# Two heads by turns: reordering the small attention matmuls of a decoder block

## The chip, the core and the metric

The kernel runs on one core of a Trainium2 chip. TensorE (PE in the rows, PEld for its weight loads), VectorE (DVE), ScalarE (ACT), GpSimdE (POOL) and the DMA queues started by SyncE (SP) each run a queue of their own and meet at semaphores. The metric is the device time of one execution in microseconds. Over three runs the kernel before took 1109.73, 1112.56 and 1114.26 us, median 1112.56.

## The reference, cut to what matters

One decoder layer over 256 tokens of width 1024, in float32: a conditioned norm, an input projection, two attentions that are gated and merged, an output projection, then an expert network in which every token meets 16384 experts' grid, and a last norm. The change touches only the two attentions. Both have heads of 64 columns.

```python
# stick-breaking attention, 8 heads
z = einsum('bqhd,bkhd->bhqk', qb, kb) * scale            # scores, contraction over 64
log_1m_beta = where(mask, log_sigmoid(-z), 0)
after = cumsum(log_1m_beta, reverse=True) - log_1m_beta
a = where(mask, exp(log_sigmoid(z) + after), 0)
out = einsum('bhqk,bkhd->bqhd', a, vb)                   # weighted values, 64 columns out
...
# dilated attention, 4 heads in each of 3 groups, softmax over the three groups' keys together
z = einsum('bqhd,bqnhd->bhqn', qb, kg) * scale
out = einsum('bhqn,bqnhd->bqhd', softmax(z), vg)
```

## The kernel before, in words

Everything dense runs as three float32r matmuls per product (a high and a low part of each operand; helper `mm3`, lines 85 to 87), whose weights come from DRAM in blocks of 512 KB (`unit`); ACT copies the high part out (line 81) and DVE subtracts to get the low part (line 82). A gate projection `gates(b)` is two such blocks, 48 matmuls.

The attentions use plain float32 matmuls, which the trace shows as two matmul records each. Two heads of 64 rows lie in one 128-partition tile: an even head in partitions 0 to 63, an odd one in 64 to 127.

- `stick_a(p)`, for a pair p of four: the scores of two heads go to two PSUM banks of one tile `z`. For each head a bf16 matmul over all 128 rows writes the mask (line 358), then the scores add to it: one float32 matmul with 256 moving columns (line 359) and one with 128 (line 363), both on the 64 rows of the head. The second head follows when the first is done.
- `stick_b(p)` adds the running sums (lines 377, 378), full-size float32 matmuls.
- `stick_c(p)`: weighted values, 64 output columns per head, so head 0 writes partitions 0 to 63 of the tile `po` and head 1 partitions 64 to 127 (lines 388, 392). Head 0's two matmuls come first in the code, then head 1's, with nothing between.
- `dilated(h, o)`, for one head at a time: for each half `tt` of the queries the masks (line 404, or 407 and 408), three score matmuls on the head's 64 rows (line 411) with 128 or 256 moving columns, the softmax (DVE maximum line 417, ACT exponential line 421, DVE scaling line 423), transposes in threes (line 428) that ACT copies out (line 429), and three or six weighted-value matmuls with 64 output columns (line 433) into the head's half of the tile `o`. The scores' tile is one of two buffers of pool `pz`, which the projections of the values (`proj_v`) use too; the transposes' tile and `o` share two buffers of pool `pm`, so the transposes have one of them.

At the end of the attention stage a loop takes two pairs of dilated heads; after each head come two gate projections and, with `bg`, one step of background work on DVE.

A planner at build time lays out each engine's queue. It takes instructions by their place in the code, but passes over those that it reckons not to be ready, so that the transposes stand in the trace amid the gate projections that follow them in the code.

Of the kernel before, what the change touches and what calls it, by code (L numbers as in the profile page):

```python
# [7 lines left out]
F32 = mybir.dt.float32  # L8
# [4 lines left out]
AF = mybir.ActivationFunctionType  # L13
# [11 lines left out]
# activations of the first J0 columns of experts are worked out while the routing goes on and kept in DRAM  # L25
J0 = 116
# steps of the routing, and batches of gates, to a pair of such columns
PACE_R = 2.5
PACE_G = 2.0
# the first norm's scales (even) and shifts (odd) that the tensor engine works out  # L30
# [4 lines left out]
def kernel(  # L35
# [60 lines left out]
    def rsqrt(r, m, q, n=1):  # L96
        # 1 / sqrt(m) for n columns, halves m: first guess from the exponent, then Newton steps to float32's
        # accuracy
        nc.vector.tensor_scalar(r.bitcast(I32), m.bitcast(I32), 1, None, op0=OP.arith_shift_right)
        nc.vector.tensor_scalar(  # L100
            r.bitcast(I32), r.bitcast(I32), -1, 0x5F3759DF, op0=OP.mult, op1=OP.add
        )
        nc.vector.tensor_scalar(m, m, -0.5, None, op0=OP.mult)
        for _ in range(3):
            for i in range(n):
                c = slice(i, i + 1)
                nc.vector.scalar_tensor_tensor(q[:, c], r[:, c], r[:, c], m[:, c], op0=OP.mult, op1=OP.mult)
            for i in range(n):
                c = slice(i, i + 1)
                nc.vector.scalar_tensor_tensor(r[:, c], q[:, c], 1.5, r[:, c], op0=OP.add, op1=OP.mult)  # L110
# [51 lines left out]
    def ada1(k):  # L162
        # scale and shift of row block k; some from the weights as they come on the tensor engine
        raw = spool.tile([P, 2, D], F32, tag="ada", bufs=3, name=f"ada1_{k}")
        nc.sync.dma_start(raw, w_ada[2 * k : 2 * k + 2].rearrange("k p d -> p k d"))
        got = []
        for i in range(2):
            t = 2 * k + i
            if t in ON_PE:
                row = pp.tile([1, P], F32, tag="pp", name=f"row_{t}")  # L170
                wk = raw[:, i].rearrange("p (k n) -> p k n", k=NC8)
                for j in range(NC8):
                    nc.tensor.matmul(row, cc[:, j : j + 1], wk[:, j], start=(j == 0), stop=(j == NC8 - 1))
                rs = spool.tile([1, P], F32, tag="rs", bufs=2, name=f"rs_{t}")
                nc.scalar.activation(rs, row, AF.Copy, scale=-1.0)
                cm = pm.tile([P, 1], F32, tag="mm", name=f"cm_{t}")
                nc.tensor.matmul(cm, rs, neg_one[0:1, 0:1], start=True, stop=True)
                got.append(cm)
            else:
                dots(raw[:, i : i + 1], t)  # L180
                got.append(mod[:, t : t + 1])
        g, b = gs[:, 0, k : k + 1], mod[:, 2 * k + 1 : 2 * k + 2]
        nc.vector.scalar_tensor_tensor(
            g, got[0], bcol1[:, k : k + 1], gcol[:, 0, k : k + 1], op0=OP.add, op1=OP.mult
        )
        nc.vector.tensor_add(b, got[1], bcol[:, 2 * k + 1 : 2 * k + 2])
        return g, b
# [10 lines left out]
    def rms(sq, name):  # L198
        # 1 / rms with tokens on partitions, then along them on all partitions
# [37 lines left out]
    # the first column blocks, for q and k, take each row block of h as its modulation arrives  # L237
# [72 lines left out]
    def roped(dst, ps, name):  # L310
        t1 = spool.tile([P, 2, T], F32, tag="att", bufs=6, name=f"t1_{name}")
        t2 = spool.tile([P, 2, T], F32, tag="att", bufs=6, name=f"t2_{name}")
        nc.vector.tensor_mul(t1, ps, rp[:, 0:1].to_broadcast([P, 2, T]))
        nc.vector.tensor_mul(t2, ps, rp[:, 1:2].to_broadcast([P, 2, T]))
        # rows of a pair of tiles: heads 0 2 1 3; two heads of 64 rows to each tile that is kept
        for i in range(2):
            nc.vector.tensor_sub(dst[:, i], t1[:, 0], t2[:, 1])
        for i, to, at in ((0, 32, 0), (0, 96, 64), (1, 0, 32), (1, 64, 96)):
            nc.vector.tensor_add(dst[to : to + 32, i], t2[at : at + 32, 0], t1[at : at + 32, 1])
# [33 lines left out]
    def stick_a(p):  # L353
        z = pz.tile([P, 2, 512], F32, tag="z", name=f"z{p}")
        for h in range(2):
            hs = slice(64 * h, 64 * h + 64)
            zt = z[:, h, 0:384].rearrange("p (a t) -> p a t", a=3)
            nc.tensor.matmul(z[:, h, 0:384], ident_b, sb_mask, start=True, stop=False)
            nc.tensor.matmul(
                zt[:, 0:3:2], k_sb[hs, p, 0:P], q_sb[hs, p].rearrange("p (a t) -> p a t", a=2),  # L360
                start=False, stop=False,
            )
            nc.tensor.matmul(zt[:, 1], k_sb[hs, p, P:T], q_sb[hs, p, P:T], start=False, stop=True)
# [18 lines left out]
    def stick_c(p, a):  # L382
        o = pm.tile([P, T], F32, tag="mm", name=f"po{p}")
        for h in range(2):
            hs = slice(64 * h, 64 * h + 64)
            cs_ = slice(128 * p + 64 * h, 128 * p + 64 * h + 64)
            at = a[:, h].rearrange("p (a t) -> p a t", a=3)
            nc.tensor.matmul(
                o[hs].rearrange("p (a t) -> p a t", a=2), v_sb[:, 0, cs_], at[:, 0:3:2],
                start=True, stop=False,  # L390
            )
            nc.tensor.matmul(o[hs, P:T], v_sb[:, 1, cs_], at[:, 1], start=False, stop=True)
        put_o(o, p, f"sb{p}")

# [1 line left out]
    def dilated(h, o):  # L396
        hs = slice(64 * (h % 2), 64 * (h % 2) + 64)
        for tt in range(2):
            ts_ = slice(P * tt, P * tt + P)
            n = 1 + tt  # L400
            z = pz.tile([P, 1024], F32, tag="z", name=f"zd{h}_{tt}")
            if tt == 0:
                zt = z[:, 0:384].rearrange("p (g s) -> p g s", g=3)
                nc.tensor.matmul(zt, ident_b, dil_mask[:, :, P:T], start=True, stop=False)
            else:
                zt = z[:, 0:768].rearrange("p (g s) -> p g s", g=3)
                nc.tensor.matmul(zt[:, 0:2], ident_b, dil_mask[:, 0:2], start=True, stop=False)
                nc.tensor.matmul(zt[:, 2], ident_b, dil_mask[:, 2], start=True, stop=False)
            for g in range(3):
                i = 2 * g + h // 2  # L410
                nc.tensor.matmul(
                    zt[:, g], q_d[hs, i, ts_], k_d[hs, i, 0 : P * n],
                    start=False, stop=(g == 2 or (g == 1 and tt == 1)),
                )
            zf = z[:, 0 : 384 * n]
            mx = spool.tile([P, 4], F32, tag="mx", bufs=2, name=f"mx{h}_{tt}")
            anchor[:] = [nc.vector.tensor_reduce(mx[:, 0:1], zf, AX, OP.max)]
            nc.vector.tensor_scalar(mx[:, 1:2], mx[:, 0:1], -0.125, None, op0=OP.mult)
            pr = spool.tile([P, 768], F32, tag="att", bufs=6, name=f"pr{h}_{tt}")
# [4 lines left out]
            pT = spool.tile([P, 6, P], F32, tag="att", bufs=6, name=f"pT{h}_{tt}")  # L424
            for i0 in range(0, 3 * n, 3):
                pt = pm.tile([P, 3, P], F32, tag="mm", name=f"pt{h}_{tt}_{i0}")
                for i in range(3):
                    nc.tensor.transpose(pt[:, i], pf[:, (i0 + i) * P : (i0 + i + 1) * P], ident)
                nc.scalar.activation(pT[:, i0 : i0 + 3], pt, AF.Copy)
            oh = slice(64 * (h % 2), 64 * (h % 2) + 64)  # L430
            for i in range(3 * n):
                g, st = divmod(i, n)
                nc.tensor.matmul(
                    o[oh, ts_], v_d[:, st, 256 * g + 64 * h : 256 * g + 64 * h + 64], pT[:, i],
                    start=(i == 0), stop=(i == 3 * n - 1),
                )
# [32 lines left out]
    for p in range(2):  # L469
        o = pm.tile([P, T], F32, tag="mm", name=f"pd{p}")  # L470
        for h in range(2):
            dilated(2 * p + h, o)
            for i in range(2):
                gates(4 * p + 2 * h + i)
                bg()
# [98 lines left out]
    sel_pool = es_s.enter_context(tc.tile_pool(name="sel", bufs=1, side="right"))  # L574
    # per slot (head, rank): both halves of its expert's number, its gate in three parts
# [22 lines left out]
    # x1 with tokens on partitions, for the end  # L598
# [21 lines left out]
    for tt in range(2):  # L620
# [17 lines left out]
        # pairs (a, b) of ranks with (a + 1) * (b + 1) > 16 have 16 pairs before them, so  # L638
        # a < 4 with every b and a >= 4 with b < 4 hold the 16 best, in the order of a * 16 + b
# [69 lines left out]
    def grid_mm(b, A, Bs):  # L709
        # a gate's parts add up to it without error  # L710
# [102 lines left out]
    # 1 / sqrt(sum / D + EPS) is sqrt(D) / sqrt(sum + D * EPS), and sqrt(D), a power of two, is in gfb  # L813
# [38 lines left out]
def _arrays(inputs):  # L852
# [11 lines left out]
    # scale and shift of the first norm by turns, then gate 1, scale 2, shift 2, gate 2; all transposed but  # L864
    # for those that the tensor engine works out
# [65 lines left out]
```

## Time and profile before

| what | value |
|---|---|
| median of three runs | 1112.56 us (1109.73 to 1114.26) |
| span of the profiled execution | 1112.9 us |
| PE busy | 1077.8 us (97%) |
| DVE busy | 833.5 us (75%) |
| ACT busy | 557.8 us (50%) |
| DMA | 237.58 MB, mean 213 GB/s |
| chain that ended last | PE 60%, DMA 9%, DVE 8% |
| line 411, dilated scores | 48 records, 10.0 us busy |
| line 433, dilated weighted values | 72 records, 10.0 us busy |
| lines 359 and 363, stick-breaking scores | 16 and 16 records |

The profiled execution's span is 1112.9 us, 0.3 us over the median of the runs; no time of it outside the span is shown. The attention stages lie between about 54 and 218 us. Matmul records overlap, since one begins before the one ahead has ended, so what a matmul costs is read from the distance of starts and not from its length.

### The profile page before, as it was taken

The page shows a single profiled execution, that of the slowest core. Times are in us where ns is not written, and L with a number is a line of the kernel's source. Part 1 is how long each engine was busy: PE and PEld are TensorE (multiplying, and loading weights), DVE is VectorE, ACT ScalarE, POOL GpSimd, SP SyncE. Part 2 cuts the span into 40 slices and gives each one's busy share as a digit, 9 for nine tenths or more (in the row PEclk, how much of TensorE's full clock was granted, in tenths as well). Part 3 has the DMA queues.
Part 4 walks back from the last instruction along what each step waited for, and adds up shares of the span by engine and source line. Part 5 has one row for each costly group of instructions (what it writes and reads, how often), then busy time and mean ns, then how long its engine had stood idle before and what let it go on. Part 6 is the DMA issues. An engine that isn't in the chain of part 4 may idle for free.

```text
span 1112.9 us, 19549 instructions
## 1 busy us (share of the span) xinstructions
PE 1077.8 (97%) x7671; PEld 984.2 (88%) x7674; DVE 833.5 (75%) x1539; ACT 557.8 (50%) x706; POOL 0.2 (0%) x4
## 2 busy tenths in 40 slices
PE   6899999999999999999999999999999999999986
PEld 4878988998999999999999999988887878888865
DVE  6777877686699889877877777677676767676675
ACT  4476344564465545554454544544444444445432
POOL 0000000000000000000000000000000000000000
PEclk9999999999999999999999999999999999999998
DMA  9954566453976765765555555576766667768751
GB/s 336 362 195 175 173 220 223 153 174 125 333 258 209 232 218 198 247 208 176 187 181 180 190 178 177 178 246 220 232 210 236 217 237 232 236 223 274 253 200 38
DMA packets 74206, 237.58 MB, mean 213 GB/s; under 512 B 8449, under 2 KB 8833, under 8 KB 73986
## 3 DMA queue, kind: packets, MB, share of 16 engines
q1 hardware_dynamic: 64898, 220.04, 58.7%
q10 hardware_dynamic: 9216, 16.29, 4.0%
q8 instruction: 60, 0.98, 0.4%
q14 instruction: 32, 0.26, 0.1%
HBM read 219.00 MB, written 17.30 MB: 212 GB/s over the span
## 4 chain that ended last, share of the span: by engine, by line
PE 60%; DMA 9%; DVE 8%; issue 3%; ACT 1%; DVEq 0%; SPq 0%; ACTq 0%
PE pus L85 9%; PE pus L86 8%; PE pus L87 8%; DMA a<-act_spill 8%; PE acc L87 6%; PE acc L86 6%; PE acc L85 6%; PE pg L714 4%; DVE wl L82 2%; DVE l_v L82 2%; PE p_pq L85 1%; PE p_pq L86 1%; PE p_pq L87 1%; DVE l_u L82 1%; DMA act_spill<-as 1%
## 5 line engine op out<-in xcount | busy, mean ns | idle before, releaser
L85 PE MATMUL pus<-hh_n,h_u 128*128 128x256 f32 x928 | 265.7, 286 | 0.0
L86 PE MATMUL pus<-hl_n,h_u 128*128 128x256 f32 x928 | 262.6, 283 | 0.0
L87 PE MATMUL pus<-hh_n,l_u 128*128 128x256 f32 x928 | 262.4, 283 | 0.0
L81 ACT ACTIVATE h_u<-r_u 128x1024 fp32r<-128x1024 f32 x128 | 135.5, 1060 | 180.9 <-PE pus L86 150.3
L87 PE MATMUL acc<-h_v,wl 128*128 128x512 f32 x512 | 201.3, 393 | 2.0 <-DVE wl L82 1.5
L86 PE MATMUL acc<-l_v,wh 128*128 128x512 f32 x512 | 200.9, 392 | 0.6 <-DVE l_v L82 0.6
L85 PE MATMUL acc<-h_v,wh 128*128 128x512 f32 x512 | 200.1, 391 | 0.0
L81 ACT ACTIVATE h_v<-r_v 128x1024 fp32r<-128x1024 f32 x128 | 135.0, 1056 | 119.1 <-PE acc L87 53.3
L82 DVE TENSOR_TENSOR l_u<-r_u,h_u 128x1024 fp32r<-128x1024 f32 x128 | 155.2, 1219 | 30.8 <-ACT h_u L81 30.5
L86 PEld LDWEIGHTS pus<-hl_n,h_u 128*128 128x128 f32 x928 | 178.0, 192 | 0.0
L87 PEld LDWEIGHTS pus<-hh_n,l_u 128*128 128x128 f32 x928 | 177.9, 192 | 0.0
L85 PEld LDWEIGHTS pus<-hh_n,h_u 128*128 128x128 f32 x928 | 177.8, 192 | 0.0
L82 DVE TENSOR_TENSOR l_v<-r_v,h_v 128x1024 fp32r<-128x1024 f32 x128 | 154.3, 1220 | 15.3 <-ACT h_v L81 15.1
L764 DVE TENSOR_TENSOR a<-a,G 128x512 f32<-128x512 f32 x64 | 70.3, 1099 | 99.0 <-DMA a<-act_spill 99.0
L87 PEld LDWEIGHTS acc<-h_v,wl 128*128 128x128 f32 x512 | 96.5, 189 | 26.1 <-DVE wl L82 6.3
L86 PEld LDWEIGHTS acc<-l_v,wh 128*128 128x128 f32 x512 | 96.7, 189 | 22.0 <-DVE l_v L82 2.1
L85 PEld LDWEIGHTS acc<-h_v,wh 128*128 128x128 f32 x512 | 96.6, 189 | 19.5
L730 DVE TENSOR_TENSOR B<-E,selT 128x768 bf16<-128x768 bf16 x128 | 68.1, 552 | 33.1 <-PE pg L714 33.1
L81 ACT ACTIVATE wh<-a 128x512 fp32r<-128x512 f32 x64 | 40.4, 631 | 78.3 <-PE acc L86 69.9
L151 DVE SCALAR_TENSOR_TENSOR junk<-ada,c_sb 128x1024 bf16<-128x1024 f32 x44 | 53.5, 1217 | 2.5 <-DMA ada<-in_w_ada_dram 2.2
L714 PE MATMUL pg<-B,A 128*128 128x128 bf16 x768 | 52.0, 222 | 0.1
L714 PEld LDWEIGHTS <-A 128*128 128x128 bf16 x768 | 46.9, 114 | 1.6
(319 smaller groups left out, 1837.9 us busy)
## 6 DMA issues: line engine op xcount, KB each, us to landing
r_u<-in_u_dram SPq DMA_DIRECT2D x128, 512.0 KB, 3.9
r_v<-in_v_dram SPq DMA_DIRECT2D x128, 512.0 KB, 4.4
ada<-in_w_ada_dram SPq DMA_DIRECT2D x20, 1024.0 KB, 7.3
act_spill<-as ACTq DMA_DIRECT2D x58, 256.0 KB, 2.5
a<-act_spill SPq DMA_DIRECT2D x58, 256.0 KB, 3.7
r_g<-in_w_in_dram SPq DMA_DIRECT2D x16, 512.0 KB, 3.6
r_pq<-in_w_pq_dram SPq DMA_DIRECT2D x16, 512.0 KB, 6.0
r_first<-in_w_in_dram SPq DMA_DIRECT2D x8, 512.0 KB, 7.4
```

The source lines that it names most:

```text
L81: nc.scalar.activation(hi, src, AF.Copy)
L82: last_split[:] = [nc.vector.tensor_sub(lo, src, hi.bitcast(F32))]
L85: nc.tensor.matmul(ps, lh, rh, start=start, stop=False)
L86: nc.tensor.matmul(ps, lh, rl, start=False, stop=False)
L87: nc.tensor.matmul(ps, ll, rh, start=False, stop=stop)
L151: nc.vector.scalar_tensor_tensor(junk, raw[:, k], 1.0, c_sb, op0=OP.mult, op1=OP.mult, accum_out=mod[:, t + k : t + k + 1])
L714: nc.tensor.matmul(ps[:, t], A[:, :, t], Bs[t // 2][:, x, :, t % 2], start=(x == 0), stop=(x == 2))
L730: nc.vector.tensor_tensor(B, E[:, None, :, 2 * q : 2 * q + 2].to_broadcast([P, 3, P, 2]), g, op=OP.mult)
L764: nc.vector.tensor_mul(a, a, G[:, :, j : j + 2].rearrange("p t s -> p s t"))
```

## The change

In `stick_a` both masks are written first, and then the score matmuls are issued by turns: head 0, head 1, head 0, head 1. In `stick_c` the weighted-value matmuls take turns in the same way. `dilated` now takes a pair of heads and one half of the queries: masks of both heads (two `z` buffers), scores by turns, both softmaxes; it returns a function `rest` that does the transposes of both heads and then the weighted-value matmuls by turns. The loop calls `dilated`, one gate projection, `rest`, and another gate projection, for each half. No arithmetic changes: the same matmuls run on the same operands. Some comments are dropped besides.

```diff
     def stick_a(p):
         z = pz.tile([P, 2, 512], F32, tag="z", name=f"z{p}")
         for h in range(2):
-            hs = slice(64 * h, 64 * h + 64)
-            zt = z[:, h, 0:384].rearrange("p (a t) -> p a t", a=3)
             nc.tensor.matmul(z[:, h, 0:384], ident_b, sb_mask, start=True, stop=False)
-            nc.tensor.matmul(
-                zt[:, 0:3:2], k_sb[hs, p, 0:P], q_sb[hs, p].rearrange("p (a t) -> p a t", a=2),
-                start=False, stop=False,
-            )
-            nc.tensor.matmul(zt[:, 1], k_sb[hs, p, P:T], q_sb[hs, p, P:T], start=False, stop=True)
+        for last in range(2):
+            for h in range(2):
+                hs = slice(64 * h, 64 * h + 64)
+                zt = z[:, h, 0:384].rearrange("p (a t) -> p a t", a=3)
+                if last:
+                    nc.tensor.matmul(zt[:, 1], k_sb[hs, p, P:T], q_sb[hs, p, P:T], start=False, stop=True)
+                else:
+                    nc.tensor.matmul(
+                        zt[:, 0:3:2], k_sb[hs, p, 0:P], q_sb[hs, p].rearrange("p (a t) -> p a t", a=2),
+                        start=False, stop=False,
+                    )
...
+    def dilated(p, o, tt):
...
         for h in range(2):
...
+            z = pz.tile([P, 1024], F32, tag="z", name=f"zd{p}{h}_{tt}")
...
+        for g in range(3):
+            for h in range(2):
+                i = 2 * g + p
                 nc.tensor.matmul(
-                    zt[:, g], q_d[hs, i, ts_], k_d[hs, i, 0 : P * n],
+                    zts[h][:, g], q_d[hss[h], i, ts_], k_d[hss[h], i, 0 : P * n],
                     start=False, stop=(g == 2 or (g == 1 and tt == 1)),
                 )
...
+        def rest():
+            for h in range(2):
+                pT, pf = pTs[h]
+                for i0 in range(0, 3 * n, 3):
+                    pt = pm.tile([P, 3, P], F32, tag="mm", name=f"pt{p}{h}_{tt}_{i0}")
+                    for i in range(3):
+                        nc.tensor.transpose(pt[:, i], pf[:, (i0 + i) * P : (i0 + i + 1) * P], ident)
+                    nc.scalar.activation(pT[:, i0 : i0 + 3], pt, AF.Copy)
             for i in range(3 * n):
                 g, st = divmod(i, n)
-                nc.tensor.matmul(
-                    o[oh, ts_], v_d[:, st, 256 * g + 64 * h : 256 * g + 64 * h + 64], pT[:, i],
-                    start=(i == 0), stop=(i == 3 * n - 1),
-                )
+                for h in range(2):
+                    c0 = 256 * g + 128 * p + 64 * h
+                    nc.tensor.matmul(
+                        o[hss[h], ts_], v_d[:, st, c0 : c0 + 64], pTs[h][0][:, i],
+                        start=(i == 0), stop=(i == 3 * n - 1),
+                    )
+        return rest
...
     for p in range(2):
         o = pm.tile([P, T], F32, tag="mm", name=f"pd{p}")
-        for h in range(2):
-            dilated(2 * p + h, o)
-            for i in range(2):
-                gates(4 * p + 2 * h + i)
-                bg()
+        for tt in range(2):
+            rest = dilated(p, o, tt)
+            gates(4 * p + 2 * tt)
+            bg()
+            rest()
+            gates(4 * p + 2 * tt + 1)
+            bg()
         put_o(o, 4 + p, f"d{p}")
```

## Rows read from the trace of the kernel before

**Rows 1.** Stretches: length, busy us (count) of PE, PEld, DVE, ACT, POOL, clock, DMA.

```profile
54.00:112.00 58.00, 54.64 (x377) 47.32 (x376) 42.48 (x61) 43.24 (x53) 0.00 (x0) 0.97 0.54 191
143.00:218.00 75.00, 74.38 (x552) 66.17 (x554) 52.84 (x97) 34.19 (x56) 0.00 (x0) 1.00 0.60 199
...
310.00:700.00 390.00, 389.93 (x3606) 388.55 (x3606) 325.69 (x827) 205.86 (x261) 0.00 (x0) 1.00 0.61 201
```

**Rows 2.** Timeline of PE, 77.9 to 81.3: start us, length us, instruction, count.

```profile
77.97 0.66 PE L388 MATMUL po<-a,v_sb 128*64 128x256 f32 x4
78.45 0.40 PE L392 MATMUL po<-a,v_sb 128*64 128x128 f32 x4
78.78 0.34 PE L358 MATMUL z<-mk 128*128 128x384 bf16 x1
79.04 0.70 PE L359 MATMUL z<-q_sb,k_sb 64*128 64x256 f32 x2
...
79.89 0.34 PE L358 MATMUL z<-mk 128*128 128x384 bf16 x1
...
81.00 0.59 PE L377 MATMUL z<-sp,tri 128*128 128x384 f32 x1
```

**Rows 3.** Timeline of PE, 143.1 to 147: head 0's scores, then a gate projection.

```profile
143.14 0.34 PE L404 MATMUL zd<-mk 128*128 128x384 bf16 x1
143.41 0.93 PE L411 MATMUL zd<-k_d,q_d 64*128 64x128 f32 x6
144.27 0.39 PE L407 MATMUL zd<-mk 128*128 128x512 bf16 x1
...
144.70 1.56 PE L411 MATMUL zd<-k_d,q_d 64*128 64x256 f32 x6
146.19 0.39 PE L85 MATMUL p_g<-hh_n,h_g 128*128 128x256 f32 x1
146.41 0.28 PE L86 MATMUL p_g<-hl_n,h_g 128*128 128x256 f32 x1
146.53 0.28 PE L87 MATMUL p_g<-hh_n,l_g 128*128 128x256 f32 x1
```

**Rows 4.** Timeline of PE, 148.8 to 156.2: head 0's weighted values and transposes.

```profile
149.05 0.87 PE L433 MATMUL pd<-pT,v_d 128*64 128x128 f32 x6
149.85 0.38 PE L86 MATMUL p_g<-hl_n,h_g 128*128 128x256 f32 x1
...
152.58 0.49 PE L428 MATMUL pt<-ident,pr 128*128 128x128 f32 x3
...
153.65 0.55 PE L428 MATMUL pt<-ident,pr 128*128 128x128 f32 x3
154.12 1.52 PE L433 MATMUL pd<-pT,v_d 128*64 128x128 f32 x12
155.58 0.39 PE L86 MATMUL p_g<-hl_n,h_g 128*128 128x256 f32 x1
```

**Rows 5.** Timeline, all engines, 24 to 33: the first projections.

```profile
24.07 1.21 DVE L82 TENSOR_TENSOR f_k_d<-r_first,f_q_d 128x1024 fp32r<-128x1024 f32 x1
...
27.57 0.39 PE L86 MATMUL p_first<-hl_n,h_first 128*128 128x256 f32 x1 [0.45 <-DVE hl_n L270]
...
32.17 0.28 PE L85 MATMUL p_first<-hh_n,f_q_d 128*128 128x256 f32 x1
```

**Rows 6.** Timeline of ACT, 143 to 145.

```profile
143.34 0.60 ACT L339 ACTIVATE v_d<-p_vd 128x512 f32<-128x512 f32 x1 [1.82 <-PE p_vd L87]
```

**Rows 7.** Waits of PE, 52 to 143: who waited for whom, us, times, longest.

```profile
PE z L358 <- ACT v_sb L330: 0.7, 1, 0.7
```

**Rows 8.** Groups of instructions, 140 to 220: busy us, mean ns, idle before.

```profile
L417 DVE TENSOR_REDUCE mx<-zd 128x1 f32<-128x384 f32 (+1 forms) x8 | 6.1, 758 | 6.7 <-PE zd L411 6.7
L421 ACT ACTIVATE pr<-zd,mx 128x384 f32<-128x384 f32 (+1 forms) x8 | 5.9, 737 | 4.7 <-DVE mx L418 4.7
L423 DVE TENSOR_SCALAR pr<-pr,mx 128x384 f32<-128x384 f32 (+1 forms) x8 | 4.1, 516 | 0.0
```

More of the change, by code (lines that the diff above doesn't have):

```diff
@@ L383, in stick_c @@
         o = pm.tile([P, T], F32, tag="mm", name=f"po{p}")
-        for h in range(2):
-            hs = slice(64 * h, 64 * h + 64)
-            cs_ = slice(128 * p + 64 * h, 128 * p + 64 * h + 64)
-            at = a[:, h].rearrange("p (a t) -> p a t", a=3)
-            nc.tensor.matmul(
-                o[hs].rearrange("p (a t) -> p a t", a=2), v_sb[:, 0, cs_], at[:, 0:3:2],
-                start=True, stop=False,
-            )
-            nc.tensor.matmul(o[hs, P:T], v_sb[:, 1, cs_], at[:, 1], start=False, stop=True)
@@ L393, in stick_c @@
[L393 to L401, printed above, removed]
+        for last in range(2):
+            for h in range(2):
+                hs = slice(64 * h, 64 * h + 64)
+                cs_ = slice(128 * p + 64 * h, 128 * p + 64 * h + 64)
+                at = a[:, h].rearrange("p (a t) -> p a t", a=3)
+                if last:
+                    nc.tensor.matmul(o[hs, P:T], v_sb[:, 1, cs_], at[:, 1], start=False, stop=True)
+                else:
+                    nc.tensor.matmul(
+                        o[hs].rearrange("p (a t) -> p a t", a=2), v_sb[:, 0, cs_], at[:, 0:3:2],
+                        start=True, stop=False,
+                    )
@@ L402, in dilated @@
+        put_o(o, p, f"sb{p}")
+    def dilated(p, o, tt):
+        hss = [slice(64 * h, 64 * h + 64) for h in range(2)]
+        ts_ = slice(P * tt, P * tt + P)
+        n = 1 + tt
+        zs, zts, pTs = [], [], []
+        for h in range(2):
+            z = pz.tile([P, 1024], F32, tag="z", name=f"zd{p}{h}_{tt}")
+            zt = z[:, 0 : 384 * n].rearrange("p (g s) -> p g s", g=3)
             if tt == 0:
-                zt = z[:, 0:384].rearrange("p (g s) -> p g s", g=3)
                 nc.tensor.matmul(zt, ident_b, dil_mask[:, :, P:T], start=True, stop=False)
@@ L405, in dilated @@
             else:
-                zt = z[:, 0:768].rearrange("p (g s) -> p g s", g=3)
                 nc.tensor.matmul(zt[:, 0:2], ident_b, dil_mask[:, 0:2], start=True, stop=False)
                 nc.tensor.matmul(zt[:, 2], ident_b, dil_mask[:, 2], start=True, stop=False)
-            for g in range(3):
-                i = 2 * g + h // 2
+            zs.append(z)
+            zts.append(zt)
+        for g in range(3):
+            for h in range(2):
+                i = 2 * g + p
                 nc.tensor.matmul(
-                    zt[:, g], q_d[hs, i, ts_], k_d[hs, i, 0 : P * n],
+                    zts[h][:, g], q_d[hss[h], i, ts_], k_d[hss[h], i, 0 : P * n],
@@ L413, in dilated @@
                     start=False, stop=(g == 2 or (g == 1 and tt == 1)),
                 )
-            zf = z[:, 0 : 384 * n]
-            mx = spool.tile([P, 4], F32, tag="mx", bufs=2, name=f"mx{h}_{tt}")
+        for h in range(2):
+            zf = zs[h][:, 0 : 384 * n]
+            mx = spool.tile([P, 4], F32, tag="mx", bufs=2, name=f"mx{p}{h}_{tt}")
             anchor[:] = [nc.vector.tensor_reduce(mx[:, 0:1], zf, AX, OP.max)]
             nc.vector.tensor_scalar(mx[:, 1:2], mx[:, 0:1], -0.125, None, op0=OP.mult)
-            pr = spool.tile([P, 768], F32, tag="att", bufs=6, name=f"pr{h}_{tt}")
+            pr = spool.tile([P, 768], F32, tag="att", bufs=6, name=f"pr{p}{h}_{tt}")
@@ L423, in dilated @@
             nc.vector.tensor_scalar(pf, pf, mx[:, 3:4], None, op0=OP.mult)
[L424 to L430, printed above, removed]
+            pT = spool.tile([P, 6, P], F32, tag="att", bufs=6, name=f"pT{p}{h}_{tt}")
+            pTs.append((pT, pf))
+        def rest():
+            for h in range(2):
+                pT, pf = pTs[h]
[4 more added lines that the diff above has]
+                    nc.scalar.activation(pT[:, i0 : i0 + 3], pt, AF.Copy)
             for i in range(3 * n):
                 g, st = divmod(i, n)
-                nc.tensor.matmul(
-                    o[oh, ts_], v_d[:, st, 256 * g + 64 * h : 256 * g + 64 * h + 64], pT[:, i],
-                    start=(i == 0), stop=(i == 3 * n - 1),
-                )
+                for h in range(2):
+                    c0 = 256 * g + 128 * p + 64 * h
+                    nc.tensor.matmul(
+                        o[hss[h], ts_], v_d[:, st, c0 : c0 + 64], pTs[h][0][:, i],
+                        start=(i == 0), stop=(i == 3 * n - 1),
+                    )
+        return rest
     nc.sync.dma_start(mk, msk)
```

## The prediction

> **What bounds the kernel now.** I read the table of stretches first. Between 54 and 112 us, where the stick-breaking attention runs, PE is busy 54.64 of 58.00 us; between 143 and 218, where the dilated attention runs beside the gate projections, 74.38 of 75.00; in the long expert stretch behind, 389.93 of 390.00 [rows 1]. No other engine comes near: DVE has 52.84 of 75.00 us in the dilated stretch, ACT 34.19. What PE saves there is therefore saved in the end, unless one of its few waits grows. In the timelines of PE I then looked at distances of starts, since the lengths overlap.
>
> What the reader should see there are two things. First, a float32 matmul over 64 rows has half the array idle: the group of six score records with 128 columns fills 143.41 to 144.27, 0.86 us, and the one with 256 columns 144.70 to 146.19, 1.49 us [rows 3]. The difference, 0.63 us for 6 x 128 more columns, is 0.105 us per record and 128 columns, so 0.23 us of each group (0.86 - 0.63) is a fixed price for going into the 64-row form and out of it. Second, two heads' matmuls can already run side by side, and do so: in `stick_c` four records of 256 columns take 77.97 to 78.45, 0.48 us, or 0.12 us each, where 64-row records of that width cost 0.21; and the code puts head 0's two matmuls ahead of head 1's, yet the four of line 388 stand before the four of line 392 [rows 2]. The chip took the other half's work out of the order of the code.
>
> The Trainium skill (TensorE: Matmul & The Clock Gate, "What overlaps and what doesn't") says that matmuls start and end strictly in program order. By that rule `stick_c` would run its heads one after the other now and the change would gain about 0.6 us on each of four pairs, an estimate (one head's 2 x 0.21 + 2 x 0.105); rows 2 show otherwise, and the measurement decides.
>
> **The change part by part.**
>
> `stick_c`: the heads overlap already, so I take nothing. Its bounds are 0 and, if the turns closed what is left at the edges (0.81 us from 77.97 to 78.78, less the 0.63 of one head), 4 x 0.18 = 0.7 us.
>
> `stick_a`: between the heads stands a mask over the full array, so the heads cannot meet. One pair takes 78.78 to 81.00, 2.22 us: mask 0.26, scores 0.85 (79.04 to 79.89), mask 0.27, scores the rest [rows 2]. After the change the two masks stand together. A dense 256-column matmul follows its neighbour after 0.12 us (146.41 to 146.53), so a mask of 384 columns that is followed by another costs about 0.18 us, and the second 0.26: 0.44 us [rows 3]. Then one score group. If the heads overlap fully it is 0.85 us, in all 1.29, and 0.9 us is saved per pair, 3.6 us in four. If they don't overlap, head 1's 6 x 0.105 = 0.63 us comes on top and the pair saves 0.3 us, 1.2 in four. No row of this kernel has 64-row matmuls of two heads next to each other; the nearest rows are the 64-column ones of `stick_c`, which overlap, so I take 3.6. Part of the first pair's saving is lost: the next pair's mask waited 0.7 us for ACT's copy `v_sb` already [rows 7], and ACT is the busiest helper there, 43.24 of 58.00 us [rows 1]; I take off 0.3.
>
> Dilated scores: for 128 columns one head costs 0.27 (mask) + 0.86 = 1.13 us, two 2.26; after, 0.18 + 0.27 + 0.86 = 1.31, saving 0.95. For 256 columns one head costs 0.43 + 1.49 = 1.92, two 3.84; after, the first head's 768 mask columns at 0.12 per 256 cost 0.36, so 0.36 + 0.43 + 1.49 = 2.28, saving 1.56 [rows 3]. Twice both is 5.0 us. Without overlap 0.63 and 1.26 come back: 2 x (0.32 + 0.30) = 1.2. One of these four groups will not pair: two heads now need both buffers of `pz` at once, and at the first one the second buffer still holds the last value projection, which ACT copies until 143.34 + 0.60 = 143.94 [rows 6], while PE wants it at 143.3. PE has head 0's scores ready then and will run them alone. I take off the whole 0.95, leaving 4.05; the bounds are 0.9 and 5.0.
>
> Weighted values of the dilated heads: 72 records. Six take 149.05 to 149.85, 0.80 us, twelve 154.12 to 155.58, 1.46 us [rows 4], so 0.11 us a record and 0.14 fixed per group. Here one head stood alone, and now its neighbour's 64 columns lie beside it, the form that overlaps in rows 2. 36 steps instead of 72 save 36 x 0.11 = 4.0 us. Each group also costs its 0.14 and about 0.10 on the matmul behind it (146.19 to 146.41 is 0.22 where 0.12 is usual [rows 3]); at least eight groups become four to six, 0.5 to 1.0 us, and I take 0.5: 4.5 us.
> This needs the heads really by turns. The queue's order is the planner's, which passes over what is not ready, and head 1's transposes end later than head 0's. But both heads write one bank of `o`, and for one bank the planner seems to keep the code's order: the weights `f_k_d` of the sixth first projection were ready at 24.07 + 1.21 = 25.3 us and PE idled 0.45 us before 27.57, yet their first matmul comes at 32.17, after those of the block that shares the bank [rows 5]. If it did not hold here, these 4.5 us would be 0.
>
> Transposes, copies, softmax instructions, DMAs and background steps are the same in number. The order of weight loads on SP's queue and of the background steps does not change either.
>
> **The sum.** 3.6 - 0.3 + 4.05 + 4.5 = 11.85 us. From the profiled execution's 1112.9 that leaves 1101.05; its span is 0.3 us above the median of the runs, 1112.56, so I expect 1100.7 us.
>
> The Trainium skill (TensorE: Matmul & The Clock Gate, "Measured speedup vs the span model") gives 3.07 times for four 32-row tiles, not 4. An estimate from that page, 1.54 times for two, would hide 0.70 of the second head's score time instead of all of it, on 4 x 0.63 + 0.63 + 2 x 1.26 = 5.7 us of such time: 1.7 us less gain. No run here shows it yet.
>
> **The rivals.**
>
> *Halves by rows do not overlap.* Only fewer changes of form are saved: 1.2 in `stick_a`, 0.9 in the dilated scores, and the 4.5 of the weighted values: 6.6 us, 1106.0 us. For it: no row has such a pair. Against it: the other split of the array overlaps, and the heads write different banks.
>
> *Weighted values do not pair.* The planner issues head 0's when its copies are done, and gate matmuls come between: 3.6 - 0.3 + 4.05 = 7.35 us, 1105.2 us. Against it rows 5, for it only that the heads are ready some 2 us apart (two rounds of 152.58 to 153.65, 1.07 us each [rows 4]).
>
> *The gain is given back.* PE reaches its next input earlier and waits: on ACT in the stick-breaking stretch, where rows 1 leave ACT 14.8 us in 58, or on DVE in the dilated stretch, where 52.84 us of work would have to go into about 66. With the queues replanned as well, 1108 to 1113. Against it: the waits of PE are few now.
>
> *Slower: the softmax of two heads is laid bare.* `rest` needs both heads' maxima, exponentials and scalings, by their means 0.76 + 0.74 + 0.52 = 2.0 us a head [rows 8], some 3 us for two that follow each other, then for 256 columns four rounds of transposes through one buffer, 4 x 1.07 = 4.3 us: 7.3 us after the scores. Weight splitting and background steps queue ahead on DVE; with five of them at 1.2 us (the length of the split in rows 5) it is about 13. In front of it and behind it stand two gate projections, 2 x 48 x 0.12 = 11.5 us of PE work. So a shortfall of about 1.8 us in each wide group is conceivable. To turn the sum round and reach slower by 0.5% (5.6 us), it would have to be (11.85 + 5.6) / 4 = 4.4 us in every one of the four groups, with PE idle; then about 1118.
>
> **How the numbers follow.** My forecast has 0.55, rows not overlapping 0.15, weighted values not pairing 0.10, given back 0.13, slower 0.07. A measurement of this kernel can tell 0.5%, 5.6 us, from no change, so "faster" is below 1107.0. The forecast lies there; of the two middle rivals, which are 0.9 to 1.8 us inside that border, I count 0.19 of 0.25; the given-back case is "same", with the other 0.06. That makes 0.74, 0.19 and 0.07. Downwards the bounds (0.7 in `stick_c`, 5.0 for the scores, 1.0 for the groups) allow 2.15 us more, 1098.6, and the queues planned anew some 3 us either way; upwards the range takes in both middle rivals and the start of the given-back case: 1095 to 1109.
>
> **What would show it.** In `stick_a` the records of lines 359 and 363 must start in pairs a few hundredths of a microsecond apart and the pair's stretch shrink from 2.22 to about 1.3 us; twelve dilated score records with 256 columns must fit into about 1.5 us; 24 weighted-value records into about 1.5 us, in one or two groups. The stretch from the first mask of the dilated heads to the end of the gate projections should fall from 75 to about 66 us, with the expert stretch as long as before. Starts of the two heads one behind the other at 0.1 or 0.2 us would prove the first rival, line 433 in groups of one head the second, and PE idle ahead of lines 428 or 433 the last. The forecast is wrong if the attention stretches shrink by less than 8 us or the rest of the span grows by several.

## The result

The changed kernel takes 1100.2 us in the median of four runs (1099.64 to 1100.88), the kernel before 1113.17 us (four runs, the three named above among them); the ratio is 0.9884, with a 95% interval of 0.9864 to 0.9904. The forecast was 1100.7 us. A second series gave 0.9878 (0.9863 to 0.9893).

The page of the profiled execution of the changed kernel, span and part 1 (busy time, share, instructions):

```profile
span 1098.9 us, 19552 instructions
PE 1063.5 (97%) x7672; PEld 973.4 (89%) x7674; DVE 832.3 (76%) x1539; ACT 557.4 (51%) x706; POOL 0.2 (0%) x4
```

Before, PE was busy 1077.8 us, with 7671 matmul records and the same 7674 weight loads: the work is the same and only laid out otherwise. The line numbers move: the masks of the stick-breaking scores are now line 356, the scores 365 and 363, the weighted values 397 and 395; the dilated masks 413, 415, 416, scores 423, transposes 446, weighted values 452.

The third pair of the stick-breaking scores in the timeline of PE after (start us, length us, instruction, merged count), with the weighted values ahead of it:

```profile
74.68 0.65 PE L397 MATMUL po<-a,v_sb 128*64 128x256 f32 x4
75.16 0.39 PE L395 MATMUL po<-a,v_sb 128*64 128x128 f32 x4
75.48 0.50 PE L356 MATMUL z<-mk 128*128 128x384 bf16 x2
75.91 0.70 PE L365 MATMUL z<-q_sb,k_sb 64*128 64x256 f32 x4
76.45 0.39 PE L363 MATMUL z<-q_sb,k_sb 64*128 64x128 f32 x4
76.76 0.59 PE L382 MATMUL z<-sp,tri 128*128 128x384 f32 x1
```

The pair takes 75.48 to 76.76, 1.28 us, where it took 2.22 [rows 2]. The eight score records, four of each width, fill 75.91 to 76.76, 0.85 us, just what the four of one head filled before: the second head costs nothing. In the single records of the trace the two heads start in pairs, less than 0.01 us apart. The weighted values above them still take 0.80 us (0.81 before), since they overlapped already.

The first group of the dilated scores, and then a wide one, timeline of PE after:

```profile
137.92 0.34 PE L413 MATMUL zd<-mk 128*128 128x384 bf16 x1
138.19 0.93 PE L423 MATMUL zd<-k_d,q_d 64*128 64x128 f32 x6
139.05 0.34 PE L413 MATMUL zd<-mk 128*128 128x384 bf16 x1
139.32 0.93 PE L423 MATMUL zd<-k_d,q_d 64*128 64x128 f32 x6
140.18 0.39 PE L85 MATMUL p_g<-hh_n,h_g 128*128 128x256 f32 x1
...
154.92 1.57 PE L423 MATMUL zd<-k_d,q_d 64*128 64x256 f32 x12
156.41 0.38 PE L85 MATMUL p_g<-hh_n,h_g 128*128 128x256 f32 x1
```

The first group is not paired: head 0's mask and scores, then head 1's, 1.13 us each, as one head cost before [rows 3]. The wide group has both heads' twelve records from 154.92 to 156.41, 1.49 us, what six cost before.

The weighted values of the first wide half, timeline of PE after:

```profile
164.85 0.43 PE L452 MATMUL pd<-pT,v_d 128*64 128x128 f32 x2
165.22 0.39 PE L86 MATMUL p_g<-hl_n,h_g 128*128 128x256 f32 x1
...
167.22 1.52 PE L452 MATMUL pd<-pT,v_d 128*64 128x128 f32 x22
168.68 0.39 PE L85 MATMUL p_g<-hh_n,h_g 128*128 128x256 f32 x1
```

Two records of head 0 go out alone at 164.85, then gate matmuls and transposes, then the other 22 from 167.22 to 168.68, 1.46 us: as long as twelve records of one head took [rows 4]. This lone pair stands in all four groups, and it leaves head 1's last two records alone at the end of each.

Where the time went is read from three starts: the first mask of the stick-breaking scores, the first mask of the dilated ones, and the first matmul of the branch projections (`brs`) behind them. Before, the outer two:

```profile
54.86 0.32 PE L358 MATMUL z<-mk 128*128 128x384 bf16 x1 [0.43 <-ACT q_sb L323]
...
218.06 0.28 PE L85 MATMUL brs<-o_hi,h_sbo 128*128 128x256 f32 x1
```

and after:

```profile
54.44 0.48 PE L356 MATMUL z<-mk 128*128 128x384 bf16 x2 [0.43 <-ACT q_sb L323]
...
205.37 0.28 PE L85 MATMUL brs<-o_hi,h_sbo 128*128 128x256 f32 x1
```

The dilated heads begin at 143.14 before [rows 3] and 137.92 after, above. This gives, with the same three starts and the end of the last instruction in the traces of the experiments below:

| kernel | stick-breaking stretch | dilated stretch | from `brs` to the end |
|---|---|---|---|
| before | 88.28 | 74.91 | 894.8 |
| changed | 83.49 | 67.45 | 893.5 |
| stick-breaking part alone | 83.50 | 74.95 | 896.3 |
| dilated part alone | 88.25 | 67.48 | 895.5 |
| no turns in the scores | 83.52 | 68.56 | 896.7 |
| both heads on one half | 85.42 | 70.43 | 895.6 |
| changed, second series | 83.50 | 67.45 | 896.5 |
| values head by head | 83.50 | 70.23 | 895.4 |
| last copy first | 83.49 | 65.70 | 895.6 |
| last copy first, values' projection earlier | 83.50 | 65.85 | 896.4 |

So 4.8 us come from the first stretch and 7.5 from the second, and they come again to a few hundredths in every kernel that has the same code there. The last stretch differs by up to 3 us between executions in which nothing of it is changed, the changed kernel's own two included (893.5 and 896.5); its 1.3 us of gain in the profile of after is such scatter, and no part of the effect. A part of the scatter is the granted clock, as the first experiment shows.

### The profile page after: what moved, and what is told of

It is laid out like the page before. It is cut to its first block, busy times and chain, and to the rows that moved or that the text cites. A ratio compares the mean times of both kernels' runs of the same rounds, so it can differ in the third digit from the quotient of the medians.

```text
span 1098.9 us, 19552 instructions
## 1 busy us (share of the span) xinstructions
PE 1063.5 (97%) x7672; PEld 973.4 (89%) x7674; DVE 832.3 (76%) x1539; ACT 557.4 (51%) x706; POOL 0.2 (0%) x4
## 4 chain that ended last, share of the span: by engine, by line
PE 69%; DMA 8%; DVE 5%; issue 3%; ACT 1%; DVEq 0%; SPq 0%; ACTq 0%
PE pus L85 10%; PE pus L86 10%; PE pus L87 10%; PE acc L87 7%; PE acc L86 7%; PE acc L85 7%; DMA a<-act_spill 6%; PE pg L737 4%; DVE l_v L82 1%; DVE wl L82 1%; DMA r_pq<-in_w_pq_dram 1%; PE p_g L85 1%; PE p_g L86 1%; PE pum L87 1%; PE pum L85 1%
```

## The experiments

Each experiment was timed in five rounds beside the kernel before. The first four ran on one chip (before: 1114.08 us), the last four on another (before: 1114.14 us); ratios are to the kernel before of the same series.

**The stick-breaking part alone.** The kernel before with the new `stick_a` and `stick_c`; the dilated attention and its loop are as before.

```diff
         for h in range(2):
-            hs = slice(64 * h, 64 * h + 64)
-            zt = z[:, h, 0:384].rearrange("p (a t) -> p a t", a=3)
             nc.tensor.matmul(z[:, h, 0:384], ident_b, sb_mask, start=True, stop=False)
...
+        for last in range(2):
+            for h in range(2):
+                hs = slice(64 * h, 64 * h + 64)
+                zt = z[:, h, 0:384].rearrange("p (a t) -> p a t", a=3)
...
```

> The kernel before with the new stick-breaking score and value order alone; the dilated attention is as before. Theory (the score matmuls of two heads share the array, and the stick-breaking stretch also loses a cold piece of PE's clock): the stretch from the first mask to the dilated heads' first mask shrinks by about 4.8 us (4 x 0.9 less 0.3, and 1.4 from the clock), so 1113 goes to about 1108.5. Rival (the clock's part came from somewhere else, or by chance): 3.3 us, about 1110. Rival (nothing of it is kept): 1113.

Measured: 1109.72 us, ratio 0.9955 (0.9939 to 0.9970); that is 5.0 us less than before by the ratio and 4.4 by the medians, and the interval holds the theory's 4.8 us and the rival's 3.3. The stretch decides: it is 4.78 us shorter. The clock's share is there too: the stretch 70 to 74 of before, of the changed kernel and of this one (length, busy time and count of PE, PEld, DVE, ACT, POOL, then the granted clock):

```profile
70.00:74.00 4.00, 3.71 (x20) 3.71 (x21) 1.93 (x5) 3.94 (x5) 0.00 (x0) 0.62 0.00 0
```

```profile
70.00:74.00 4.00, 4.00 (x36) 4.00 (x35) 3.63 (x5) 3.97 (x5) 0.00 (x0) 1.00 0.11 25
```

```profile
70.00:74.00 4.00, 4.00 (x35) 4.00 (x35) 3.46 (x7) 3.97 (x5) 0.00 (x0) 1.00 0.07 8
```

Before, PE waits 2.07 us in one piece for ACT's `h_qd`, until 70.29, and after it the granted clock falls: 0.62 over these 4 us, that is mostly the lower level of 1.2 GHz, and the matmuls there start 0.21 us apart instead of 0.12. In the changed kernel it is 1.00, 2.4 GHz throughout, though PE does not wait less, 3.1 us in all against 2.8, but in three pieces. Its waits from 60 to 75 (who waited for whom: us in total, times, longest):

```profile
PE z L382 <- DVE sp L376: 1.3, 1, 1.3
PE z L356 <- ACT v_sb L330: 1.0, 1, 1.0
PE p_qd L85 <- ACT h_qd L81: 0.8, 1, 0.8
```

The 48 matmuls of the second value projection stand behind that wait. Before, the wait and their first:

```profile
70.29 0.38 PE L85 MATMUL p_qd<-hh_n,h_qd 128*128 128x256 f32 x1 [2.07 <-ACT h_qd L81]
...
70.64 0.28 PE L85 MATMUL p_vs<-h_vs,hh_n 128*128 128x256 f32 x1
```

and in the changed kernel:

```profile
68.74 0.39 PE L85 MATMUL p_vs<-h_vs,hh_n 128*128 128x256 f32 x1
```

Up to the weighted values (77.97 before [rows 2], 74.68 after) that is 7.33 and 5.94 us, 1.39 us less.

The cold piece stands in both traces with the old stick-breaking functions (before, and the next kernel) and in none of the eight with the new ones. Over all runs the mean granted clock is 0.990 before and in the next kernel, 0.993 in this one and 0.991 to 0.994 in the others with the new functions. But the length of a wait does not settle whether the clock falls behind it. With both heads on one half (below) PE waits 1.7 us for `h_qd` in one piece, 2.7 us in all, and keeps its clock of 1.00. And behind `brs`, where nothing is changed, the two profiles of the changed kernel have the same waits from 240 to 254 (1.1, 0.9, 0.6 and 0.3 us); then the first keeps its clock and the second, of the second series, does not:

```profile
254.00:257.00 3.00, 3.00 (x27) 3.00 (x27) 3.00 (x9) 1.40 (x4) 0.00 (x0) 1.00 0.00 0
```

```profile
254.00:257.00 3.00, 3.00 (x16) 3.00 (x16) 2.80 (x8) 1.81 (x5) 0.00 (x0) 0.50 0.00 0
```

So the same code with the same waits can go either way from one execution to the next, and the 1.4 us are a gain that the traces show, not one that a shorter wait is sure to bring.

**The dilated part alone.** The changed kernel with the old `stick_a` and `stick_c`.

```diff
         for h in range(2):
+            hs = slice(64 * h, 64 * h + 64)
+            zt = z[:, h, 0:384].rearrange("p (a t) -> p a t", a=3)
             nc.tensor.matmul(z[:, h, 0:384], ident_b, sb_mask, start=True, stop=False)
...
-        for last in range(2):
-            for h in range(2):
...
```

> The changed kernel with the old stick-breaking functions. Theory (the two parts add up): the dilated stretch shrinks by about 7.5 us as in the changed kernel and the stick-breaking stretch by nothing, cold clock included, so about 1105.5. Rival (the parts share one gain, or the later stages give it back): under 4 us, above 1109.

Measured: 1106.67 us, ratio 0.9934 (0.9910 to 0.9958). The dilated stretch is 7.43 us shorter, the other one unchanged, cold clock included; the same window of 70 to 74:

```profile
70.00:74.00 4.00, 4.00 (x26) 4.00 (x25) 2.43 (x4) 3.96 (x5) 0.00 (x0) 0.65 0.00 0
```

The parts add up: 0.45% and 0.66% make 1.11%, the whole change 1.16 to 1.22%. The rival that the gain is given back falls.

**No turns.** The changed kernel, its masks still ahead, but each score group and the stick-breaking weighted values head by head.

```diff
-        for last in range(2):
-            for h in range(2):
+        for h in range(2):
+            for last in range(2):
...
-        for g in range(3):
-            for h in range(2):
+        for h in range(2):
+            for g in range(3):
```

> The changed kernel with the masks still ahead but every score group, and the stick-breaking weighted values, issued head by head (all of head 0, then all of head 1). Theory (the chip itself takes the other half's matmuls forward, so standing next to each other is enough): the same time as the changed kernel within 0.5 us, about 1100.2, with records of both heads starting in pairs. Rival (the turns in the code are needed): head 1's passes come on top, 4 x 0.63 + 0.63 + 2 x 1.26 = 5.7 us, about 1106.

Measured: 1105.07 us, ratio 0.9924 (0.9900 to 0.9949). Time alone settles nothing: the interval just touches that of the changed kernel (0.9864 to 0.9904), and the median lies near the rival's 1106. The two stretches are together only 1.1 us longer than the changed kernel's; the other 3 us lie behind `brs` (896.7 against 893.5), where nothing differs, and where this trace has a granted clock of 0.51 from 251 to 258. The trace shows each theory half right. Stick-breaking scores, third pair, and a wide dilated group, timeline of PE:

```profile
75.83 0.71 PE L365 MATMUL z<-q_sb,k_sb 64*128 64x256 f32 x4
76.36 0.39 PE L363 MATMUL z<-q_sb,k_sb 64*128 64x128 f32 x4
76.69 0.59 PE L382 MATMUL z<-sp,tri 128*128 128x384 f32 x1
...
154.87 2.10 PE L423 MATMUL zd<-k_d,q_d 64*128 64x256 f32 x12
156.90 0.39 PE L85 MATMUL p_g<-hh_n,h_g 128*128 128x256 f32 x1
```

With four records of head 0 ahead the chip pairs the heads itself: 75.83 to 76.69 is 0.86 us, as with turns. That this is the chip and not the planner is told by the program as it is built: its queue for TensorE holds the heads one after the other, as the code does, and the same is so for `stick_c` in the kernel before. With six ahead the pairing is only partial: the twelve records take 154.87 to 156.90, 2.03 us, against 1.49 with turns and about 2.8 one after the other (next experiment). In all three such groups head 1's first record starts less than 0.01 us behind head 0's third. The dilated stretch grows by 1.1 us. So for the stick-breaking scores standing next to each other is enough; the turns help where three matmuls of a head follow one another, by 1.1 us in all.

**Both heads on one half.** The changed kernel, but head 1's scores read head 0's 64 rows, so that its scores are not its own.

```diff
-                hs = slice(64 * h, 64 * h + 64)
+                hs = slice(0, 64)
...
-                    zts[h][:, g], q_d[hss[h], i, ts_], k_d[hss[h], i, 0 : P * n],
+                    zts[h][:, g], q_d[hss[0], i, ts_], k_d[hss[0], i, 0 : P * n],
```

> The changed kernel, but both heads' score matmuls read head 0's 64 rows, so both use the same half of the array; order, sizes and counts are as in the changed kernel. The second head's scores are therefore not its own. Theory (the gain of the scores is the other half of the array): the passes run one after the other, 4 x 0.63 + 0.63 + 2 x 1.26 = 5.7 us more than the changed kernel, about 1106. Rival (the gain comes from fewer changes between 64-row and full form and from the new order): the same as the changed kernel, about 1100.

Measured: 1108.61 us, ratio 0.9947 (0.9930 to 0.9963), clear of the changed kernel's interval. The same two groups, timeline of PE:

```profile
75.82 1.13 PE L365 MATMUL z<-q_sb,k_sb 64*128 64x256 f32 x4
76.79 0.60 PE L363 MATMUL z<-q_sb,k_sb 64*128 64x128 f32 x4
77.32 0.59 PE L382 MATMUL z<-sp,tri 128*128 128x384 f32 x1
...
156.13 2.85 PE L423 MATMUL zd<-k_d,q_d 64*128 64x256 f32 x12
```

The eight records now take 75.82 to 77.32, 1.50 us instead of 0.85, and the twelve wide ones 2.85 us long instead of 1.57. The stretches grow by 1.9 and 3.0 us, 4.9 of the expected 5.7; in the first one PE's waits from 60 to 80 are 0.4 us shorter (2.7 us against 3.1), which takes up part of the rest. The order and the changes of form are those of the changed kernel, so the gain of the scores is the second half of the array.

**The values head by head.** In `rest`, all weighted values of head 0, then all of head 1. (The changed kernel itself ran beside this and the next two.)

> The changed kernel itself, unchanged, run beside the next three for comparison: 0.988 of the kernel before.

```diff
-            for i in range(3 * n):
-                g, st = divmod(i, n)
-                for h in range(2):
+            for h in range(2):
+                for i in range(3 * n):
+                    g, st = divmod(i, n)
```

> The changed kernel, but the dilated weighted values are issued head by head: all of head 0, then all of head 1. Theory (turns in the code keep the heads together, because head 0's records otherwise go out as soon as its own copies are done): for 256 keys the heads fall apart into groups of six records at 0.8 us, 4 x 0.8 + some 0.2 against 0.36 + 1.45 us in the changed kernel, so 2 x 1.6 = 3.2 us more; for 128 keys they stay together and lose nothing. In all about 3 us more than the changed kernel. Rival (the chip pairs them whatever the code says): no difference.

Measured: the changed kernel 1101.20 us, ratio 0.9878; this one 1104.99 us, 0.9910 (0.9895 to 0.9926). The dilated stretch is 2.78 us longer. A wide group, timeline of PE:

```profile
165.25 0.87 PE L452 MATMUL pd<-pT,v_d 128*64 128x128 f32 x6
166.05 0.55 PE L446 MATMUL pt<-ident,pr 128*128 128x128 f32 x3
166.52 0.87 PE L452 MATMUL pd<-pT,v_d 128*64 128x128 f32 x6
...
167.80 0.87 PE L452 MATMUL pd<-pT,v_d 128*64 128x128 f32 x6
...
169.38 0.87 PE L452 MATMUL pd<-pT,v_d 128*64 128x128 f32 x6
```

Head 0's six records, transposes, six more, and so on: head 0 goes out as its copies are done, and in the wide groups the pairing is lost, as expected.

**The last copy first.** The weighted values begin with what is copied last, so that nothing can go out alone.

```diff
-            for i in range(3 * n):
+            for i in reversed(range(3 * n)):
                 g, st = divmod(i, n)
-                for h in range(2):
+                for h in (1, 0):
...
-                        start=(i == 0), stop=(i == 3 * n - 1),
+                        start=(i == 3 * n - 1), stop=(i == 0),
```

> The changed kernel, but the weighted values begin with what is copied last: head 1 ahead of head 0, and the key blocks from the last to the first. Theory (each of the four groups now loses 0.36 us and 0.1 at the gate matmul behind to one matmul of head 0 that goes out alone, two records, while head 1's copy is awaited): four groups of one piece, 4 x 0.46 = 1.8 us less than the changed kernel, about 0.987 of the kernel before. Rival (the later start costs as much as the lone matmul): no difference, or PE idle ahead of line 452.

Measured: 1100.50 us, ratio 0.9866 (0.9847 to 0.9884). One group, timeline of PE:

```profile
168.13 1.53 PE L452 MATMUL pd<-pT,v_d 128*64 128x128 f32 x24
169.59 0.39 PE L85 MATMUL p_g<-hh_n,h_g 128*128 128x256 f32 x1
```

All 24 records stand together, 1.46 us, the dilated stretch is 1.75 us shorter than that of the changed kernel, and PE waits for nothing new (0.2 us in the dilated stretch, as in the changed kernel). The stretch bears the theory out. By time the two kernels are 0.7 us apart with intervals that overlap, so that it is faster is likely and not shown.

**And the values' projection earlier.** The last copy first, and the last value projection moved ahead of the last two of q and k, so that both score buffers are free.

```diff
     vd(1)
+    vd(2)
     qd(2)
     kd(2)
-    vd(2)
```

> The kernel of the last-copy-first order, with the last value projection also issued two projections earlier, so that both score buffers are free when the dilated heads begin. Theory (the first score group of the dilated heads runs unpaired, 2.26 us, only because the second buffer is still held): both heads pair there, 0.6 to 0.95 us less than the last-copy-first kernel. Rival (something else holds head 1 back): its first scores still run alone, no difference.

Measured: 1102.14 us, ratio 0.9887 (0.9872 to 0.9902): the forecast gain of 0.6 to 0.95 us did not come. The start of the dilated scores, timeline of PE:

```profile
138.46 0.50 PE L413 MATMUL zd<-mk 128*128 128x384 bf16 x2
138.89 0.71 PE L423 MATMUL zd<-k_d,q_d 64*128 64x128 f32 x8
...
142.49 0.93 PE L423 MATMUL zd<-k_d,q_d 64*128 64x128 f32 x4 [0.18 <-DVE k_d L319]
```

The mask pair and eight records of both heads stand together now: the buffer was what kept head 1 back. But the last four come 3.6 us later, behind DVE's rope of the last k projection (`k_d`), at the price of one more change of form, and the stretch is no shorter (65.85 against 65.70).

## Why the prediction was right

- **The bound.** PE had no slack in either stretch, and what it saved there was saved in the end; the parts alone add up to the whole. In the changed kernel PE waits 0.2 us in the whole dilated stretch (for DVE's `pr`), so neither the softmax nor DVE was laid bare, and the two last rivals fall.
- **`stick_c`, nothing.** 0.80 us against 0.81. The trace of before did show that the chip takes the other half's matmuls out of the order of its queue, and the kernel without turns shows it for halves by rows too (0.86 us for eight records). The Trainium skill (TensorE: Matmul & The Clock Gate, "What overlaps and what doesn't") has matmuls in strict program order; these rows differ from it.
- **`stick_a`, 3.6 less 0.3.** The pair's 1.28 us answer to the 1.29 forecast. The 0.3 came true as well, in part by chance: the wait for `v_sb` grew from 0.7 to 1.0, a new one of 1.3 for DVE's `sp` came, and the one for `h_qd` shrank from 2.1 to 0.8. The stretch gave 4.8. The term that was missing is the clock: the prediction names neither the 2.1 us wait for `h_qd` nor the cold piece behind it, 1.4 us, though the granted clock of 0.97 in [rows 1] holds it. That it went away with the stick-breaking part is shown by the two kernels that have one part each; why the clock fell behind that wait and not behind the others stays open.
- **Dilated scores, 4.05.** The first group stayed unpaired, for the reason given: the last kernel frees the buffer and its heads pair. That halves by rows overlap was taken over from halves by columns; the kernel with both heads on one half shows it. The score records' busy time falls from 10.0 us (line 411) to 5.9 (line 423, below), 4.1 us; some mask records are missing in both profiles, so that theirs is not summed here.
- **Weighted values, 4.5.** Here the size was off, by about 1 us: 10.0 us busy before (line 433), 6.5 after, 3.5 saved; the dilated stretch as a whole gave 7.5 us, 3.4 beyond the scores. The groups of the changed kernel and of the one with the last copy first (busy us, mean ns of one, idle before):

```profile
L452 PE MATMUL pd<-pT,v_d 128*64 128x128 f32 x72 | 6.5, 281 | 0.1
L423 PE MATMUL zd<-k_d,q_d 64*128 64x128 f32 (+1 forms) x48 | 5.9, 341 | 0.0
```

```profile
L452 PE MATMUL pd<-pT,v_d 128*64 128x128 f32 x72 | 4.8, 278 | 0.1
```

  I had expected four to six pieces and each with two heads in it. The order within one bank was kept, as I read from [rows 5], but an order by turns that is kept lets the very first matmul, head 0's, go out before head 1 is ready; the planner put 14 other matmuls between it and head 1's first in a wide group, two in a narrow one. In each of the four groups two records at the start and two at the end go without a partner. So the 72 records take 44 steps instead of 36, in eight pieces where before there were ten (the prediction counted eight). By the prediction's own prices, 28 steps and two pieces saved are 28 x 0.11 + 2 x 0.24 = 3.6 us. With the last copy first the lone pairs are gone, four pieces of 36 steps remain, and the records take 4.8 us, 5.2 less than before.
- **Overlap in full or in part.** Two halves of 64 rows overlapped fully (0.85 us for eight records and for four). The estimate from the Trainium skill (TensorE: Matmul & The Clock Gate, "Measured speedup vs the span model"), 1.54 times for two, is not borne out here; the page's figure is for four tiles.

The mechanism was right in each part, but that the sum came within 0.5 us of the median is luck: a term left out (1.4 us of clock) and a term too large (the weighted values, by about 1 us) made up for each other. The two stretches gave 12.3 us against the 11.85 forecast, and the medians lie 13.0 us apart. One slip in the chances changes nothing: the first rival lay 1.0 us inside the border, not 0.9.

## What to carry to other kernels

In these traces, matmuls that use half of the array cost nothing beside a partner on the other half, and did not meet it where a full-array matmul stood between them in the queue. Move masks and other full-size pieces ahead of the group, and take turns where more than two matmuls per partner follow one another. When a pair's inputs come ready at different times, begin with the one that comes last, or the first matmul goes out alone and pays for a group of its own. And look at the granted clock behind the waits: where it fell, 16 matmuls started 0.21 us apart instead of 0.12, which was 1.4 us beside 3.3 us of work saved.

## What the runs showed of the hardware that was not expected

- The chip looks past earlier matmuls in its queue for work on the other half, but not far: past two float32 matmuls of the other head (four records) at no cost, 0.86 us; past three (six records) only from the third record on, 2.03 us for twelve records against 1.49 us by turns. What sets the distance is not shown.
- One wait of 2.1 us was followed by 4 us at a granted clock of 0.62 in the kernel before, and of 0.65 in the one with the dilated part alone, while waits of 1.0, 1.3 and 0.8 us in the same place left it at 1.00, and so did one of 1.7 us. The cold piece cost 1.4 us. Elsewhere the same kernel with the same waits kept its clock in one execution (1.00) and lost it in another (0.50).
